# The scan's state decay on VectorE, and ln(dt) in the bias of the mask's exponential

## The chip, the cores and the metric

The kernel runs on one core of a Trainium2 chip. The metric is the device time of one execution in microseconds (us), lower is better; a kernel's time here is the median of its runs.

## The reference, cut to what matters

One step of a one-layer hybrid encoder on 1024 prompt tokens and 64 sample tokens: a large input projection, differential attention, a state-space scan (SSD), two branch projections, an output projection, and a convolutional feed-forward part. The change lies in the scan. Per chunk of tokens it computes:

```python
acum = jnp.cumsum(dtc * a_neg, axis=1)
seg = acum[:, :, None] - acum[:, None, :]
decay = jnp.exp(jnp.where(causal[None, :, :, None, None], seg, -jnp.inf))
xdt = xc * dtc[..., None]
cb = jnp.einsum('blgn,bsgn->blsg', cc, bc)
y = jnp.einsum('blsg,blsge,bsgep->blgep', cb, decay, xdt)
y = y + jnp.einsum('blgn,bgepn->blgep', cc, state) * jnp.exp(acum)[..., None]
to_end = jnp.exp(acum[:, -1:] - acum)
state = state * jnp.exp(acum[:, -1])[..., None, None] + jnp.einsum('blgn,blge,blgep->bgepn', bc, to_end, xdt)
```

There are 32 heads in 4 groups of 8. The time step `dt` multiplies `xc` along the summed token `s`, so it may stand as a factor exp(ln dt) in `decay` just as well.

## The kernel before, in words

The layer is one program. Nearly every large product is split into high and low parts and runs as three TensorE matmuls (lines 170, 171 and 172 of `product`). After the attention comes the scan: `scan()` walks 4 groups, each of three spans (384, 384 and 320 tokens), each span in chunks of 128 tokens (the last chunk of a group is the 64 sample tokens, with a state of its own, `start`). That makes 36 chunks; a chunk's first half (`front`) runs one chunk ahead of its second half (`back`).

`front` transposes the chunk's x on TensorE into a PSUM tile `tr`, has VectorE multiply it by `dt` and by `dtw` in one instruction (L1306, out `xx` = `xdt` and `xw`), lets GpSimd write -1e30 above the diagonal of the decay's exponents `bc` (`affine_select`, L1307), takes eight exponentials on ScalarE with `nacum` as bias (L1309), and multiplies them by C·B on VectorE (L1310). `back` runs the products yi (L1318, from `xdt` and `bc`), ye (L1324, from the state) and the state's update `up` (L1330, from `xw`). VectorE multiplies ye by the outer decay (L1325) and adds yi (L1326). A group's first chunk has no state yet: ScalarE copies yi to y (L1328) and `up` to the new state (L1333). In the other 32 chunks GpSimd multiplies the old state by its decay (L1335), and VectorE adds `up` (L1337). `gated`, `normed` and `scaled` finish a span and store y to DRAM (`y_sc`, L1374 for the first two groups, L1365 for the others). The tile y has two buffers, so the first write to a span's y waits until the store of the span two before it has landed.

TensorE is kept busy between the scan's small products: after each half step `fill(SCAN_STEPS)` takes matmuls of other work, here the gate projections and then the attention and SSM branches (`branch`), whose results VectorE (L234) or ScalarE (L232, L970) takes out of PSUM. All engines run their instructions in the order in which the scheduler put them at build time; it orders by a priority and its own estimate of times, so an edit can move instructions far from its own lines. `steps()` runs once, early in the input projections, and makes `dt_tok`, `nacum`, `decs` and `dtw` for all chunks at once.

Of the kernel before, what the change touches and what calls it, by code (L numbers as in the profile page):

```python
# [9 lines left out]
F32 = mybir.dt.float32  # L10
R32 = mybir.dt.float32r
AF = mybir.ActivationFunctionType
ALU = mybir.AluOpType
# [4 lines left out]
P = 128  # L18
# [71 lines left out]
def hybrid_layer(ctx: ExitStack, tc: tile.TileContext, xT, xt, prm, cst, rope, wvd, win, wbs, wba, wout, wup, wdn,  # L90
                 ckT, cv, st0, yT, kT, v, ssm, conv, ffn):
    nc = tc.nc
    V, S, G, PE = nc.vector, nc.scalar, nc.gpsimd, nc.tensor
    act = S.activation
# [166 lines left out]
    nacum, decs = (dq.tile([P, 9, 32], F32, name=n) for n in ("nacum", "decs"))  # L261
    dtt = dq.tile([P, 2, 9, 32], F32, name="dtt")
    dt_tok, dtw = dtt[:, 0], dtt[:, 1]
# [12 lines left out]
    def stat(w):  # L276
        t = ps1.tile([P, 512], F32, name="st", tag="st")
        return t[:, :w]
# [197 lines left out]
    def row(tag, name, dt=F32):  # L476
        if tag in ("fa", "fs", "fu"):
            w = {"fa": KT * P, "fs": 4 * P, "fu": HT}[tag]
            return rows_l.tile([P, w], dt, name=name, tag=tag, bufs=IN_ROWS[tag])
        w = {"ss": T}.get(tag, HT)  # L480
        return rows_r.tile([P, w], dt, name=name, tag=tag, bufs=IN_ROWS[tag])
# [223 lines left out]
    def steps():  # L705
        flat = [four[:, 288 * i : 288 * (i + 1)] for i in range(3)] + [row("fx", "dt2")[:, :288]]
        da, e, t, t2 = (x.rearrange("p (a b) -> p a b", b=32) for x in flat)
        u = dtw
        act(e, u, AF.Abs)
        act(e, e, AF.Exp, scale=-1.0)  # L710
        V.tensor_scalar_add(t, e, 2.0)
        V.reciprocal(t, t)
        V.tensor_tensor(out=t, in0=t, in1=e, op=ALU.mult)
        V.tensor_tensor(out=t2, in0=t, in1=t, op=ALU.mult)
        yield
        V.tensor_scalar(e, t2, 1.0 / 17, None, ALU.mult)
        for n in (15, 13, 11, 9, 7, 5, 3):
            V.scalar_tensor_tensor(e, e, 1.0 / n, t2, ALU.add, ALU.mult)
        yield
        V.scalar_tensor_tensor(e, e, 1.0, t, ALU.add, ALU.mult)  # L720
        V.tensor_scalar_max(u, u, 0.0)
        V.scalar_tensor_tensor(dt_tok, e, 2.0, u, ALU.mult, ALU.add)
        an = four[:, 864:896]
        act(an, par[:, O_AL : O_AL + 32], AF.Exp)
        V.scalar_tensor_tensor(da, dt_tok, -1.0, an.unsqueeze(1).to_broadcast([P, 9, 32]), ALU.mult, ALU.mult)
        V.memset(da[TS:, 8, :], 0.0)
        yield
        flat = lambda x: x.rearrange("p a b -> p (a b)")
        pa = stat(288)
        with tc.issue_after(seen["mm"].ins):  # L730
            PE.matmul(pa, tri, flat(da), start=True, stop=True)
        V.tensor_scalar(flat(nacum), pa, -1.0, None, ALU.mult)
        yield
        pl = stat(288)
        with tc.issue_after(seen["mm"].ins):
            PE.matmul(pl, ones, flat(da), start=True, stop=True)
        act(flat(decs), pl, AF.Exp)
        V.tensor_tensor(out=flat(dtw), in0=pl, in1=flat(nacum), op=ALU.add)
        act(dtw, dtw, AF.Exp)
        V.tensor_tensor(out=dtw, in0=dtw, in1=dt_tok, op=ALU.mult)  # L740
        yield
        for c, w in WIDE:
            af = row("fc", "af")[:32, :w]
            pf = stat(512)
            with tc.issue_after(seen["mm"].ins):
                for i in range(c // P, -(-(c + w) // P)):
                    n = min(P, T - i * P)
                    PE.matmul(pf[:32, i * P - c : i * P - c + n], da[:n, i], tri[:n, :n], start=True, stop=True)
            V.tensor_copy(af, pf[:32, :w])
            m = (min(c + w, TP) - c) // P  # L750
            load(out=a_sc[c // P : c // P + m].rearrange("c h t -> h c t"), in_=af[:, : P * m].rearrange("h (c t) -> h c t", t=P))
            if c + w > TP:
                load(out=a_sc[8, :, :TS], in_=af[:, P * m : P * m + TS])
            yield
# [510 lines left out]
    with (tc.tile_pool(name="sin", bufs=1) as sin, tc.tile_pool(name="sp", bufs=1) as sp,  # L1265
# [21 lines left out]
        def front(g, ch, o, bx, xs, bc):  # L1287
            L = P if ch < 8 else TS
            cs = slice(o, o + L)
            h8 = slice(8 * g, 8 * g + 8)  # L1290
            e2 = sp.tile([P, 4, P], F32, name="e2", tag="e2", bufs=3)
            for u in range(2):
                half = slice(64 * u, 64 * u + 64)
                act(e2[half, :, :L], bc.rearrange("p (j u) t -> p u j t", u=2)[half, u, :, :L], AF.Exp)
            tr = psi.tile([P, 512], F32, name="tr", tag="tr")
            for j in range(4):
                PE.transpose(tr[:L, P * j : P * (j + 1)], xs[:, j, cs], ident)
            cb = psi.tile([P, 512], F32, name="cb", tag="cb")
            PE.transpose(cb[:L, 0:P], bx[:, 0, cs], ident)
            PE.matmul(cb[:L, P : P + L], bx[:, 0, cs], bx[:, 1, cs], start=True, stop=True)  # L1300
            b_cb = sp.tile([P, 2 * P], F32, name="b_cb", tag="b_cb", bufs=3)
            S.copy(b_cb[:L, : P + L], cb[:L, : P + L])
            xx = sp.tile([P, 2, 8, 64], F32, name="xx", tag="xx", bufs=2)
            xdt, xw = xx[:, 0], xx[:, 1]
            tr3 = tr[:L].rearrange("p (e q) -> p e q", e=8).unsqueeze(1).to_broadcast([L, 2, 8, 64])
            V.tensor_tensor(out=xx[:L], in0=tr3, in1=dtt[:L, :, ch, h8].unsqueeze(3).to_broadcast([L, 2, 8, 64]), op=ALU.mult)  # L1306
            G.affine_select(bc[:L, :, :L], bc[:L, :, :L], [[0, 8], [1, L]], ALU.is_ge, -1e30, base=0, channel_multiplier=-1)  # L1307
            for e in range(8):
                act(bc[:L, e, :L], bc[:L, e, :L], AF.Exp, bias=nacum[:L, ch, 8 * g + e : 8 * g + e + 1])  # L1309
            V.tensor_tensor(out=bc[:L, :, :L], in0=bc[:L, :, :L], in1=b_cb[:L, P : P + L].unsqueeze(1).to_broadcast([L, 8, L]), op=ALU.mult)  # L1310
            return L, cs, bc, e2, b_cb, xdt, xw

        def back(g, ch, bx, y, state, start, L, cs, bc, e2, b_cb, xdt, xw):
            h8 = slice(8 * g, 8 * g + 8)
            yi = psi.tile([P, 4, P], F32, name="yi", tag="yi")
            for e in range(8):
                u = 64 * (e % 2)
                PE.matmul(yi[u : u + 64, e // 2, :L], xdt[:L, e], bc[:L, e, :L], start=True, stop=True)  # L1318
            if ch == 8:
                state = start  # L1320
            if state is not None:
                ye = pss.tile([P, 4, P], F32, name="ye", tag="ye")
                for j in range(4):
                    PE.matmul(ye[:, j, :L], state[:, P * j : P * (j + 1)], bx[:, 1, cs], start=True, stop=True)  # L1324
                V.tensor_tensor(out=y[:, :, cs], in0=ye[:, :, :L], in1=e2[:, :, :L], op=ALU.mult)  # L1325
                V.tensor_tensor(out=y[:, :, cs], in0=y[:, :, cs], in1=yi[:, :, :L], op=ALU.add)  # L1326
            else:
                S.copy(y[:, :, cs], yi[:, :, :L])  # L1328
            up = pss.tile([P, 512], F32, name="stp", tag="stp")
            PE.matmul(up, b_cb[:L, :P], xw[:L].rearrange("p e q -> p (e q)"), start=True, stop=True)  # L1330
            new = sp.tile([P, 512], F32, name="state", tag="state", bufs=2)
            if state is None:
                S.copy(new, up)  # L1333
            else:
                G.tensor_tensor(out=new.rearrange("p (e q) -> p e q", e=8), in0=state.rearrange("p (e q) -> p e q", e=8),  # L1335
                                in1=decs[:, ch, h8].unsqueeze(2).to_broadcast([P, 8, 64]), op=ALU.mult)
                V.tensor_tensor(out=new, in0=new, in1=up, op=ALU.add)  # L1337
            if ch >= 7:
                ends.append((ssm[ch - 7, :, 512 * g : 512 * (g + 1)], new))
            return new  # L1340
# [37 lines left out]
        def scan():  # L1378
# [9 lines left out]
            def begin(n):  # L1388
                if n == len(steps):
                    return None  # L1390
                if n and n + 2 < len(steps):
                    asked.append(ask(*steps[n + 2]))
                i, g, c, w, o = steps[n]
                return front(g, (c + o) // P, o, *got[i], asked[n])
# [592 lines left out]
```

## Time and profile before

| | |
|---|---|
| median of 3 runs | 2413.97 us (2413.55 to 2416.66) |
| the profiled execution | 2411.51 us, of which the span of its instructions is 2409.7 us |
| TensorE busy, share of the span | 98% |
| VectorE, ScalarE, GpSimd busy | 72%, 50%, 26% |
| the scan | from about 1130 to 1475 us of the span |
| TensorE clock granted | 0.999 of full speed |

In rows of the profile PE is TensorE's matmul, PEld its weight load, DVE is VectorE, ACT is ScalarE, POOL is GpSimd and SP the engine that issues DMAs. A row of waits reads: engine, the waiting tile and line, `<-` what released it, then microseconds in total, number of waits, longest wait. A row on a tile reads: line, engine, operation, `x` count, then shortest, median and longest time in ns.

### The profile page before, as it was taken

What the parts mean: (1) busy time and instruction counts of PE and PEld (TensorE: products, weight loads), DVE (VectorE), ACT (ScalarE), POOL (GpSimd) and SP (SyncE); (2) the same over time, 40 slices, a digit from 0 to 9 for tenths busy, and PEclk for the clock granted to TensorE, in tenths of its full rate; (3) what the DMA queues carried; (4) which work ended last, traced back from release to release, by engine and by line L of the source; (5) the groups of instructions that cost most, each with busy time, mean ns of one, the idle gap of its engine ahead of it and who ended that gap; (6) DMA issues with size and microseconds to landing.
All of it is one profiled execution on the core that took longest, in us unless ns stands there. A gap on an engine that the chain in (4) does not pass through costs nothing. (4 is left out here: it accounts for less than half of the span.)

```text
span 2409.7 us, 48636 instructions
## 1 busy us (share of the span) xinstructions
PE 2373.4 (98%) x18649; PEld 2302.2 (96%) x18649; DVE 1729.4 (72%) x2938; ACT 1201.2 (50%) x2600; POOL 634.4 (26%) x689
## 2 busy tenths in 40 slices
PE   8999999999999999999999999999999999999998
PEld 8999999999999999999898889999899999999998
DVE  4678887646858768884898886647866667677765
ACT  6444454335656656665566664334443343353442
POOL 0032443320100000001223220012254455443444
PEclk9999999999999999999999999999999999999999
DMA  7873768526554444435978956663124324357876
GB/s 246 273 245 129 266 221 303 170 102 208 160 156 161 151 144 137 148 110 188 353 266 280 331 192 205 203 215 130 65 82 164 138 98 162 127 191 211 246 184 106
DMA packets 288170, 449.74 MB, mean 187 GB/s; under 512 B 35833, under 2 KB 178306, under 8 KB 287938
## 3 DMA queue, kind: packets, MB, share of 16 engines
q1 hardware_dynamic: 258594, 387.00, 48.6%
q0 software_dynamic: 11040, 26.34, 5.4%
q10 hardware_dynamic: 18304, 33.30, 3.7%
q8 instruction: 147, 2.41, 0.4%
q14 instruction: 85, 0.70, 0.1%
HBM read 294.03 MB, written 152.50 MB: 185 GB/s over the span
## 5 line engine op out<-in xcount | busy, mean ns | idle before, releaser
L170 PE MATMUL mm<-b,w_hi 128*128 128x272 f32 x1376 | 407.7, 296 | 0.0
L171 PE MATMUL mm<-b,w_hi 128*128 128x272 f32 x1376 | 405.8, 295 | 0.0
L172 PE MATMUL mm<-b,w_lo 128*128 128x272 f32 x1376 | 403.8, 294 | 0.0
L171 PEld LDWEIGHTS mm<-b,w_hi 128*128 128x128 f32 x1376 | 259.5, 189 | 5.9 <-issue 4.1
L170 PEld LDWEIGHTS mm<-b,w_hi 128*128 128x128 f32 x1376 | 259.3, 188 | 5.3 <-issue 2.7
L172 PEld LDWEIGHTS mm<-b,w_lo 128*128 128x128 f32 x1376 | 259.0, 188 | 5.2 <-issue 4.2
L1629 PE MATMUL mx<-m,w_hi 128*128 128x272 f32 x792 | 152.3, 289 | 2.5 <-DVE hb L1667 1.3
L420 DVE TENSOR_TENSOR wh<-w_f,wh 128x512 fp32r<-128x512 f32 (+1 forms) x156 | 149.7, 960 | 0.7 <-ACT wh L419 0.7
L1629 PE MATMUL mx<-n,wh 128*128 128x272 f32 x1056 | 141.7, 288 | 1.3 <-DVE u L1656 0.9
L1629 PEld LDWEIGHTS mx<-n,wh 128*128 128x128 f32 x1056 | 135.7, 188 | 1.7 <-DVE u L1656 1.2
L1132 ACT ACTIVATE p_t<-sc,mx 128x512 f32<-128x512 f32 (+6 forms) x144 | 106.0, 739 | 59.0 <-DVE mx L1123 33.0
L1629 PEld LDWEIGHTS mx<-m,w_hi 128*128 128x128 f32 x792 | 124.4, 188 | 2.9 <-DVE hb L1667 1.5
L170 PE MATMUL mx<-b,w_hi 128*128 128x272 f32 x416 | 123.4, 297 | 1.1 <-ACT w_hi L155 0.8
L172 PE MATMUL mx<-b,w_lo 128*128 128x272 f32 x416 | 121.6, 294 | 0.0
L563 POOL TENSOR_TENSOR ws<-w_f 128x512 f32<-128x512 f32 (+1 forms) x51 | 69.0, 1354 | 195.4 <-DMA w_f<-in_wdn_dram 84.2
L171 PE MATMUL mx<-b,w_hi 128*128 128x272 f32 x416 | 120.4, 290 | 0.0
L1009 DVE SCALAR_TENSOR_TENSOR cc<-pre,par,cc 128x544 f32<-128x544 f32 (+1 forms) x144 | 111.2, 772 | 8.2 <-ACT cc L1007 6.9
L156 DVE TENSOR_TENSOR w_lo<-w_f,w_hi 128x1024 fp32r<-128x1024 f32 (+1 forms) x74 | 92.5, 1251 | 33.9 <-ACT w_hi L155 33.7
L1629 PE MATMUL mx<-m,w_lo 128*128 128x272 f32 x396 | 114.2, 289 | 0.0
L1638 ACT ACTIVATE cc<-pre,par 128x544 f32<-128x544 f32 (+1 forms) x44 | 37.2, 846 | 150.0 <-DVE pre L1673 149.1
L419 ACT CAST wh<-w_f 128x512 fp32r<-128x512 f32 (+1 forms) x156 | 95.3, 613 | 26.1 <-POOL w_f L569 6.8
L155 ACT CAST w_hi<-w_f 128x1024 fp32r<-128x1024 f32 (+1 forms) x74 | 77.6, 1049 | 56.1 <-PE mm L171 30.3
(466 smaller groups left out, 7124.8 us busy)
## 6 DMA issues: line engine op xcount, KB each, us to landing
w_f<-in_win_dram SPq DMA_DIRECT2D x40, 512.0 KB, 3.9
w_f<-in_wup_dram SPq DMA_DIRECT2D x80, 256.0 KB, 2.6
w_f<-in_win_dram SPq DMA_DIRECT2D x76, 256.0 KB, 3.2
bc<-a_sc SPq DMA_DIRECT2D x32, 512.0 KB, 7.0
b<-y_sc SPq DMA_DIRECT2D x24, 544.0 KB, 8.2
h_sc<-hb SPq DMA_DIRECT2D x44, 272.0 KB, 2.1
ht<-h_sc SPq DMA_DIRECT2D x22, 544.0 KB, 4.6
t_sc<-ht SPq DMA_DIRECT2D x22, 544.0 KB, 3.0
```

Of the source, the lines that this page charges most:

```text
L155: S.copy(hi, w)
L156: V.tensor_tensor(out=lo, in0=w, in1=hi, op=ALU.subtract)
L170: PE.matmul(ps, a_hi, b_hi, start=i == 0, stop=False)
L171: PE.matmul(ps, a_hi, b_lo, start=False, stop=False)
L172: PE.matmul(ps, a_lo, b_hi, start=False, stop=i == n - 1)
L419: S.copy(hi, src)
L420: V.tensor_tensor(out=lo, in0=src, in1=hi, op=ALU.subtract)
L563: G.tensor_tensor(out=s1, in0=q21, in1=q22, op=ALU.add)
L1009: V.scalar_tensor_tensor(cc[:, :m], pre[:, i : i + m], cw(i), cc[:, :m], ALU.mult, ALU.add)
L1132: act(p_t[:n, :nk], sc[c][:n, :nk], AF.Exp, bias=mx[:n, c : c + 1], accum_out=dst)
L1629: PE.matmul(ps, w[x][:, c], b[y][:, k], start=start and k == i == 0, stop=k == 3 and i == 2, skip_group_check=not start)
L1638: act(cc[:, :n], pre[h][:, :n], AF.Identity, bias=col(O_FB + f), scale=cw(0))
```

## The change: what it does

```diff
--- before.py
+++ after.py
@@ -738,6 +738,9 @@
         V.tensor_tensor(out=flat(dtw), in0=pl, in1=flat(nacum), op=ALU.add)
         act(dtw, dtw, AF.Exp)
         V.tensor_tensor(out=dtw, in0=dtw, in1=dt_tok, op=ALU.mult)
+        V.tensor_scalar_max(dt_tok, dt_tok, 1e-37)
+        act(dt_tok, dt_tok, AF.Ln)
+        V.tensor_tensor(out=nacum, in0=nacum, in1=dt_tok, op=ALU.add)
         yield
         for c, w in WIDE:
             af = row("fc", "af")[:32, :w]
@@ -1302,8 +1305,9 @@
             S.copy(b_cb[:L, : P + L], cb[:L, : P + L])
             xx = sp.tile([P, 2, 8, 64], F32, name="xx", tag="xx", bufs=2)
             xdt, xw = xx[:, 0], xx[:, 1]
-            tr3 = tr[:L].rearrange("p (e q) -> p e q", e=8).unsqueeze(1).to_broadcast([L, 2, 8, 64])
-            V.tensor_tensor(out=xx[:L], in0=tr3, in1=dtt[:L, :, ch, h8].unsqueeze(3).to_broadcast([L, 2, 8, 64]), op=ALU.mult)
+            tr3 = tr[:L].rearrange("p (e q) -> p e q", e=8)
+            S.copy(xdt[:L], tr3)
+            V.tensor_tensor(out=xw[:L], in0=tr3, in1=dtw[:L, ch, h8].unsqueeze(2).to_broadcast([L, 8, 64]), op=ALU.mult)
             G.affine_select(bc[:L, :, :L], bc[:L, :, :L], [[0, 8], [1, L]], ALU.is_ge, -1e30, base=0, channel_multiplier=-1)
             for e in range(8):
                 act(bc[:L, e, :L], bc[:L, e, :L], AF.Exp, bias=nacum[:L, ch, 8 * g + e : 8 * g + e + 1])
@@ -1318,7 +1322,10 @@
                 PE.matmul(yi[u : u + 64, e // 2, :L], xdt[:L, e], bc[:L, e, :L], start=True, stop=True)
             if ch == 8:
                 state = start
+            new = sp.tile([P, 512], F32, name="state", tag="state", bufs=2)
             if state is not None:
+                V.tensor_tensor(out=new.rearrange("p (e q) -> p e q", e=8), in0=state.rearrange("p (e q) -> p e q", e=8),
+                                in1=decs[:, ch, h8].unsqueeze(2).to_broadcast([P, 8, 64]), op=ALU.mult)
                 ye = pss.tile([P, 4, P], F32, name="ye", tag="ye")
                 for j in range(4):
                     PE.matmul(ye[:, j, :L], state[:, P * j : P * (j + 1)], bx[:, 1, cs], start=True, stop=True)
@@ -1328,12 +1335,9 @@
                 S.copy(y[:, :, cs], yi[:, :, :L])
             up = pss.tile([P, 512], F32, name="stp", tag="stp")
             PE.matmul(up, b_cb[:L, :P], xw[:L].rearrange("p e q -> p (e q)"), start=True, stop=True)
-            new = sp.tile([P, 512], F32, name="state", tag="state", bufs=2)
             if state is None:
                 S.copy(new, up)
             else:
-                G.tensor_tensor(out=new.rearrange("p (e q) -> p e q", e=8), in0=state.rearrange("p (e q) -> p e q", e=8),
-                                in1=decs[:, ch, h8].unsqueeze(2).to_broadcast([P, 8, 64]), op=ALU.mult)
                 V.tensor_tensor(out=new, in0=new, in1=up, op=ALU.add)
             if ch >= 7:
                 ends.append((ssm[ch - 7, :, 512 * g : 512 * (g + 1)], new))
```

Three edits. In `steps()`, `dt_tok` is raised to at least 1e-37, replaced by its logarithm, and added to `nacum`; so the exponentials of the mask carry the factor dt. In `front`, `xdt` is then the plain transposed x, copied out of PSUM by ScalarE, and VectorE makes `xw` alone, in half the elements. In `back`, the multiplication of the old state by its decay moves from GpSimd to VectorE and in front of the sums of y. GpSimd keeps the `affine_select`. The tile `new` is now taken ahead of the products of the state, in every chunk.

The scheduler gives new orders to all engines within the scan; TensorE's instructions are the same in number, and their order outside the scan is unchanged. In rows of the order, what stands in brackets is whose progress the instruction waits for (Activation is ScalarE, Pool GpSimd, DMAHW a DMA queue). VectorE at the second and third chunk of the first group, before:

```order
L1325 TENSOR_TENSOR y<-ye,e_14151 128x4x128 [waits PE_49]
L1310 TENSOR_TENSOR bc<-bc,b_cb 128x1024 [waits Activation_49,Pool_49]
L1337 TENSOR_TENSOR state<-state,stp 128x512 [waits PE_49,Pool_49]
L1326 TENSOR_TENSOR y<-y,yi 128x4x128 [waits DVE_49,PE_49]
L1306 TENSOR_TENSOR xx<-tr,dtt 128x1024
L1325 TENSOR_TENSOR y<-ye,e_14260 128x4x128 [waits PE_49]
L1310 TENSOR_TENSOR bc<-bc,b_cb 128x1024 [waits Activation_49,Pool_49]
L1337 TENSOR_TENSOR state<-state,stp 128x512 [waits PE_49,Pool_49]
L1326 TENSOR_TENSOR y<-y,yi 128x4x128 [waits DVE_49,PE_49]
L1306 TENSOR_TENSOR xx<-tr,dtt 128x1024 [waits PE_49]
```

One row on `xx` per chunk makes `xdt` and `xw` together and waits for TensorE at most or, behind others, for nothing; the state's sum waits for GpSimd. The same place now, where L1310 is the new product for `xw`, L1314 the product with the mask, L1327 the state's decay, L1332 and L1333 the sums of y, and L1341 the state's sum:

```order
L1332 TENSOR_TENSOR y<-ye,e_14155 128x4x128 [waits PE_49]
L1314 TENSOR_TENSOR bc<-bc,b_cb 128x1024 [waits Activation_49,Pool_49]
L1341 TENSOR_TENSOR state<-state,stp 128x512 [waits DVE_49,PE_49]
L1310 TENSOR_TENSOR xx<-tr,dtt 128x512 [waits Activation_49]
L1327 TENSOR_TENSOR state<-state,decs 128x512 [waits DVE_49]
L1333 TENSOR_TENSOR y<-y,yi 128x4x128 [waits PE_49]
L1314 TENSOR_TENSOR bc<-bc,b_cb 128x1024 [waits Activation_49,Pool_49]
L1332 TENSOR_TENSOR y<-ye,e_14265 128x4x128 [waits PE_49]
L1310 TENSOR_TENSOR xx<-tr,dtt 128x512 [waits Activation_49]
L1341 TENSOR_TENSOR state<-state,stp 128x512 [waits DVE_49,PE_49]
L1327 TENSOR_TENSOR state<-state,decs 128x512 [waits DVE_49]
L1333 TENSOR_TENSOR y<-y,yi 128x4x128 [waits PE_49]
```

Each row on `xx` has half the elements and now waits for ScalarE, whose copy reads the same PSUM tile; the state's decay is a row more; the state's sum no longer waits for GpSimd.

ScalarE where the third group begins, around the copy of its first chunk's y (L1328 before, L1335 now; `b_cb` is a copy from PSUM, `bc` the exponentials, `e_...` the outer decay, `zin` a cast or a square for the finished span), before:

```order
L256 ACTIVATE gn_16618<-gn_16619 128x320 [waits Activation_49]
L1302 COPY b_cb<-cb 128x256 [waits PE_49]
L1370 CAST zin<-y 128x2x320 [waits DVE_49] x2
L1302 COPY b_cb<-cb 128x256 [waits PE_49]
L1328 COPY y<-yi 128x4x128 [waits DMAHW3_49]
L1294 ACTIVATE e_16788<-bc 64x512 [waits DMAHW6_49,DVE_49]
L1294 ACTIVATE e_16788<-bc 64x512
L1302 COPY b_cb<-cb 128x256 [waits PE_49]
```

The y copy (L1328) stands behind a `b_cb` copy and a cast and waits for one DMA queue. Now, where L1309 is the new copy of `xdt` and L1339 the state's copy:

```order
L1297 ACTIVATE e_16519<-bc 64x512 [waits DMAHW5_49,DVE_49]
L1297 ACTIVATE e_16519<-bc 64x512
L1305 COPY b_cb<-cb 128x256 [waits PE_49]
L1313 ACTIVATE bc<-bc,nacum 128x128 [waits Pool_49]
L1313 ACTIVATE bc<-bc,nacum 128x128 [waits Activation_49]
L1309 COPY xx<-tr 128x512 [waits PE_49]
L1313 ACTIVATE bc<-bc,nacum 128x128 x6
L1339 COPY state<-stp 128x512 [waits DMAHW7_49,DMAHW6_49,PE_49]
L1335 COPY y<-yi 128x4x128 [waits DMAHW3_49,DVE_49,PE_49]
L1350 ACTIVATE zin<-y 128x4x320 [waits DMAHW4_49,DVE_49]
L1309 COPY xx<-tr 128x512 [waits PE_49]
```

The y copy waits for a DMA in both, and behind it there now stands a copy of `xdt` for which VectorE waits. In TensorE's order, 87 gate and branch matmuls stood between the yi products of this group's first two chunks, and now 15 do.

## The prediction

> **What bounds the kernel now.** I read the page's head first, then the busy time by stretch, then who waited for whom in the scan.
>
> ```profile
> span 2409.7 us, 48636 instructions
> PE 2373.4 (98%) x18649; PEld 2302.2 (96%) x18649; DVE 1729.4 (72%) x2938; ACT 1201.2 (50%) x2600; POOL 634.4 (26%) x689
> ```
>
> TensorE is busy for 98% of the span. The change works in the scan alone, so the question is what TensorE waits for there. The stretches (length, then busy time of PE, PEld, DVE, ACT and POOL):
>
> ```profile
> 1130.00:1475.00 345.00, 341.76 (x2781) 306.35 (x2780) 287.51 (x377) 215.65 (x521) 90.78 (x68) 1.00 0.82 276
> 1200.00:1320.00 120.00, 120.00 (x981) 108.40 (x980) 111.16 (x155) 79.93 (x185) 37.65 (x24) 1.00 0.80 266
> 1320.00:1440.00 120.00, 116.76 (x961) 104.24 (x961) 94.94 (x119) 76.65 (x189) 29.78 (x24) 1.00 0.81 280
> ```
>
> In the scan's 345 us TensorE lacks 345.00 - 341.76 = 3.2 us. VectorE has 345.00 - 287.51 = 57.5 us of idle time there, ScalarE 129.4, GpSimd 254.2. VectorE is nearest to a bound between 1200 and 1320 us, where it has only 120.00 - 111.16 = 8.8 us left. The waits of the scan name the 3.2 us:
>
> ```profile
> PE yi L1318 <- ACT y L1328: 1.9, 1, 1.9
> PE tr L1297 <- DMA in<-x_sc: 0.7, 1, 0.7
> PE yi L1318 <- DVE y L1326: 0.6, 1, 0.6
> ```
>
> Three waits in 36 chunks, 1.9 + 0.7 + 0.6 = 3.2 us. GpSimd's share in the old chain looks large, but nothing of it arrives at TensorE:
>
> ```profile
> POOL bc L1307 <- ACT e L1294: 146.4, 28, 28.9
> POOL state L1335 <- DVE state L1337: 77.4, 15, 12.6
> ACT bc L1309 <- POOL bc L1307: 16.0, 16, 3.3
> DVE state L1337 <- PE stp L1330: 1.3, 2, 1.1
> ```
>
> GpSimd waits for the others (146.4 and 77.4 us), and the VectorE sum behind its state decay (L1337) never waits for GpSimd in these rows, only 1.3 us for TensorE. So the decay that is moved was hidden, and **no gain can be larger than about 3.2 us (0.13%)**, as long as the order of TensorE's own work costs the same. It should: in the scan's order the gate and branch matmuls are interrupted by scan products 105 times before and 104 times after.
>
> **The change part by part.** In `steps()`, three more operations on 128x288, once. Their nearest rows are:
>
> ```profile
> L738 DVE TENSOR_TENSOR dtt<-st,nacum x1: 452/452/452, 215.4 to 215.4; 128x288 f32<-128x288 f32 x1
> L739 ACT ACTIVATE dtt<-dtt x1: 447/447/447, 216.3 to 216.3; 128x288 f32<-128x288 f32 x1
> 180.00:240.00 60.00, 59.37 (x454) 57.11 (x453) 48.45 (x84) 29.82 (x59) 14.09 (x11) 1.00 0.38 131
> ```
>
> Two on VectorE and one on ScalarE, 3 x 0.45 = 1.4 us in a row. TensorE's next products of `steps()` read `da` and not their results, VectorE has 11.5 of 60 us free there: 0 on the path, 1.4 us if that cover is gone. The order has no more table loads on ScalarE than before, so the logarithm adds none.
>
> In the scan, the rows that price the rest (shortest, median, longest ns):
>
> ```profile
> L1306 DVE TENSOR_TENSOR xx<-tr,dtt x36: 1206/1216/1226, 1128.8 to 1454.1; 128x1024 f32<-128x1024 f32 x32, 64x1024 f32<-64x1024 f32 x4
> L1337 DVE TENSOR_TENSOR state<-state,stp x32: 669/676/689, 1145.2 to 1469.4; 128x512 f32<-128x512 f32 x32
> L1310 DVE TENSOR_TENSOR bc<-bc,b_cb x36: 672/1214/1920, 1136.3 to 1456.7; 128x1024 f32<-128x1024 f32 x32, 64x512 f32<-64x512 f32 x4
> L1333 ACT COPY state<-stp x4: 561/567/589, 1140.0 to 1392.0; 128x512 f32<-128x512 f32 x4
> L1335 POOL TENSOR_TENSOR state<-state,decs x28: 1037/1047/3618, 1140.7 to 1454.3; 128x512 f32<-128x512 f32 x28
> ```
>
> VectorE's `xw`: 512 elements with one operand in PSUM, as L1337: 36 x (0.676 - 1.216) = -19.4 us. Its new state decay: 32 times 512 elements. The lower price is again L1337's 0.676; the upper one comes from L1310, whose operands both lie in SBUF as the decay's do and whose longest time is 1920/1214 = 1.58 times its median: 1.07 us. So 32 x 0.676 = +21.6 us, at most 32 x 1.07 = +34.2 us. I take the lower, since L1310's median is the undisturbed 1214. VectorE's sum: **+2.2 us** in 345, at most +14.8. By chunks (36 in 345 us) a third of it falls between 1200 and 1320 us: 0.8 us, at most 5.1, of the 8.8 free. It does not fill VectorE up.
>
> [...]
>
> ScalarE's copy of `xdt`: 36 x 0.567 = **+20.4 us** out of 129.4 idle. It takes a place in front of the exponentials, so it can delay them by 0.57 us a chunk; between yi and its chunk's transposes stand tens of matmuls at the usual spacing. GpSimd: some 32 x 1.05 us less at the median, worth nothing on the path.
>
> **The new wait.** `xw` now waits for ScalarE's copy, since both read the tile `tr`. Behind it on VectorE stand the state's decay, the sums of y and the branch results that free TensorE's PSUM banks. Rows of VectorE waiting for ScalarE today:
>
> ```profile
> DVE w_lo L156 <- ACT w_hi L155: 10.4, 5, 3.6
> DVE bc L1310 <- ACT bc L1309: 5.9, 5, 2.7
> ```
>
> From these, a wait costs 5.9/36 = 0.16 us per chunk, and if L156's mean wait of 2.1 us met every chunk, 36 x 2.1 = 75 us, more than VectorE's 57.5 idle. I take the nearer row, L1310, which also waits once per chunk on a ScalarE result made shortly before: 6 us in all, inside the 57.5.
>
> [...]
>
> [...]
>
> **The sum.** On the path: steps 0, decay 0, copy 0, new wait 0 so far as VectorE's idle time covers it; existing waits 3.2 us, of which the order may remove or move any. I add +0.5 us, a judgement between -3.2 and the first rival's price, since ScalarE and VectorE now wait for each other once more per chunk. The profiled execution took 2411.51 us with 1.8 us outside its span; with +0.5 it would take 2412.0. The median of the runs, 2413.97, lies 2.5 us above it, so I forecast **2414.5 us**.
>
> **The rivals.** *Slower: the y store.* The longest wait of TensorE has this origin:
>
> ```profile
> 1301.12 0.29 PE L170 MATMUL mm<-b,w_hi 128*128 128x272 f32 x1
> 1302.26 0.29 PE L170 MATMUL mm<-b,w_hi 128*128 128x272 f32 x1
> 1310.76 0.94 DVE L1371 TENSOR_TENSOR y<-y,zin 128x768 fp32r<-128x768 f32 x1
> 1324.23 0.59 ACT L1328 COPY y<-yi 128x512 f32<-128x512 f32 x1 [4.97 <-DMA y_sc<-y]
> 1324.87 1.09 PE L1318 MATMUL yi<-bc,xx 128*64 128x128 f32 x16 [1.89 <-ACT y L1328]
> DVE y L1325 <- DMA y_sc<-y: 5.2, 2, 2.9
> ```
>
> ScalarE's y copy at the third group's start waited 4.97 us for the store of y, whose last part VectorE finished at 1311.70; that is 12.5 us. TensorE had 87 matmuls (9 take 1302.26 - 1301.12 = 1.14 us, so 0.127 each, 11 us) between that chunk's yi and the next and still waited 1.89 us. Now 15 stand there, 1.9 us, and behind the y copy waits ScalarE's `xdt` copy, behind that VectorE's `xw`. If the store lands as late as before relative to its products, TensorE loses up to 11 - 1.9 = 9 us: 2423. It decides from the point where the store lands more than some 2 us behind the yi product of that group's first chunk. Against it: the scheduler also puts that span's last products earlier, before the yi product of the group before's last chunk, and 5.2 us in 2 waits on VectorE cost TensorE only 0.6 us. The same pattern on VectorE could return at other span ends.
>
> *Faster: the waits go.* If ScalarE's exponentials no longer wait the 16.0 us for GpSimd's mask, and the y sums come early enough, all 3.2 us vanish: 2413.97 - 3.2 = 2410.8. That is still within 0.2%. For a larger gain nothing in these rows has room.
>
> *VectorE full.* With the upper decay price and a wait of 1 us a chunk, the stretch from 1200 to 1320 us gets 5.1 + 12.5 = 17.6 us for 8.8 free, so some 9 us would stay on the path: 2423. The row of L1337 and the mean of L1310's waits speak against it.
>
> **How the numbers follow.** About 0.2%, 4.8 us, is what a measurement of this kernel can tell from no change. Hidden as forecast, with 0 to 4 us of new small waits or some of the 3.2 us gone: 0.76, split 0.56 for the forecast and 0.20 for the waits going. The y store: 0.13, VectorE full: 0.07; both lie above 2418.8. Faster by over 0.2% would need something these rows do not show: 0.04. The low end is the forecast of all waits gone, 2410.8; the high end takes in most of both slower cases at 2422.0.
>
> **What would show it.** Right: TensorE still within 3 to 5 us of full in the scan; `xw` near 680 ns, 36 `xdt` copies near 570 ns, decays near 680 to 700; VectorE's waits for ScalarE before `xw` below 10 us. Wrong: a TensorE wait of several us on yi at the third group's start with ScalarE's y copy named (the y store), or TensorE waits on VectorE's branch results between 1200 and 1320 us (VectorE full), or a change of time outside the scan.

## The result and the profile after

The changed kernel takes 2421.28 us (median of 10 runs, 2412.33 to 2423.28) against 2413.15 us for the kernel before (10 runs): ratio 1.0024, 95% interval 1.0012 to 1.0035. A second measurement on another occasion gave 2418.78 against 2412.74, ratio 1.0025 (1.0015 to 1.0035). So the change costs 8.1 and 6.0 us by the medians, about 0.25% by both ratios. The forecast was 2414.5 us with a range from 2410.8 to 2422.0; the time lies in the range, but on the slower side, to which the prediction gave a chance of 0.20.

The head of the page of the changed kernel:

```profile
span 2420.8 us, 48654 instructions
PE 2381.3 (98%) x18649; PEld 2308.9 (95%) x18649; DVE 1730.1 (71%) x2972; ACT 1217.8 (50%) x2637; POOL 586.8 (24%) x657
```

VectorE's busy time is what it was (1729.4 before), ScalarE has 16.6 us more, GpSimd 47.6 us less. None of the three explains a longer span. Where the time went is read from two rows on tiles: the scan's first transposition (tile `tr`) and the last product of the last span's sums of squares (tile `gst`). Behind the three durations stand the first and the last start, in us. Before, then after:

```profile
L1297 PE MATMUL tr<-con,in x144: 270/273/332, 1121.7 to 1452.9; 128*128 128x128 f32 x128, 128*64 128x128 f32 x16
L1352 PE MATMUL gst<-zin,con x24: 431/484/590, 1168.8 to 1481.3; 128*128 128x384 f32 x16, 128*128 128x320 f32 x8
```

```profile
L1300 PE MATMUL tr<-con,in x144: 269/273/331, 1122.9 to 1463.2; 128*128 128x128 f32 x128, 128*64 128x128 f32 x16
L1356 PE MATMUL gst<-zin,con x24: 430/486/591, 1169.3 to 1491.6; 128*128 128x384 f32 x16, 128*128 128x320 f32 x8
```

From the first of the one to the last of the other the scan takes 1481.3 - 1121.7 = 359.6 us before and 1491.6 - 1122.9 = 368.7 us after: 9.1 of the 11.1 us by which the two spans differ; 1.2 us of the rest stand ahead of the scan and 0.8 behind it. TensorE's waits in the changed kernel's scan, all that the view lists from 1122.8 to 1491.7 us:

```profile
PE mm L170 <- ACT w_hi L155: 1.7, 1, 1.7
PE cb L1302 <- ACT b_cb L1305: 1.7, 2, 1.0
PE yi L1322 <- ACT y L1335: 1.0, 1, 1.0
PE mm L172 <- DVE w_lo L156: 0.6, 1, 0.6
PE yi L1322 <- DVE bc L1314: 0.6, 1, 0.6
PE mx L170 <- ACT w_hi L155: 0.4, 1, 0.4
PE tr L1300 <- DVE xx L1310: 0.4, 1, 0.4
PE tr L1300 <- DMA in<-x_sc: 0.3, 1, 0.3
PE mx L172 <- DVE w_lo L156: 0.2, 1, 0.2
```

They sum to 6.9 us, where 3.2 us stood before. No single wait is large; eight of the nine rows name ScalarE or VectorE. The longest comes near 1345 us: TensorE wants the weights of a branch, and ScalarE's casts of them (`w_hi`, L155) stand behind a chunk's exponentials (L1313), which themselves waited for GpSimd's mask (2.30 us long there, where its median is 1.09). VectorE made the `xw` of that stretch at 1341.55 without any wait. ScalarE's timeline there, then TensorE's (start, length, engine, line, and in brackets the idle time ahead and what ended it):

```profile
1339.89 0.37 ACT L1305 COPY b_cb<-cb 128x256 f32<-128x256 f32 x1
1342.26 2.45 ACT L1313 ACTIVATE bc<-bc,nacum 128x128 f32<-128x128 f32 x8 [2.00 <-POOL bc L1311]
1344.62 1.98 ACT L155 CAST w_hi<-w_f 128x1024 fp32r<-128x1024 f32 x2
1345.70 0.39 PE L170 MATMUL mm<-b,w_hi 128*128 128x272 f32 x1 [1.68 <-ACT w_hi L155]
1346.65 0.39 PE L170 MATMUL mx<-b,w_hi 128*128 128x272 f32 x1 [0.43 <-ACT w_hi L155]
1348.05 0.60 PE L172 MATMUL mm<-b,w_lo 128*128 128x272 f32 x1 [0.62 <-DVE w_lo L156]
```

From 1347.3 us on, behind the first two of these waits and during the third, TensorE's granted clock is at half. The stretches of the changed kernel (length, busy time of PE, PEld, DVE, ACT and POOL, granted clock, DMA share, GB/s):

```profile
1200.00:1320.00 120.00, 119.61 (x966) 107.09 (x964) 102.69 (x152) 78.15 (x179) 14.61 (x12) 1.00 0.77 258
1320.00:1440.00 120.00, 116.34 (x924) 104.48 (x926) 93.70 (x135) 83.04 (x200) 17.44 (x13) 0.97 0.86 290
```

```profile
1348.00:1354.00 6.00, 5.95 (x26) 5.96 (x27) 5.55 (x8) 0.85 (x2) 0.00 (x0) 0.50 1.08 384
```

TensorE is "busy" for 5.95 of those 6.00 us but gets through 26 matmuls, 0.229 us each, where 0.127 is usual. A mean clock of 0.97 over 120 us is about 0.03 x 120 = 3.6 us. So of the 9.1 us, 6.9 - 3.2 = 3.7 are waits and some 3.6 the clock behind them; the other 2 are neither, and what they are stays open.

The clock episode isn't needed for the verdict. In the profiled execution of the second measurement no half clock shows there (the stretch from 1320 to 1440 us has 1.00), and these rows give 1488.4 - 1123.6 = 364.8 us, still 5.2 more than before:

```profile
L1300 PE MATMUL tr<-con,in x144: 270/272/330, 1123.6 to 1460.1; 128*128 128x128 f32 x128, 128*64 128x128 f32 x16
L1356 PE MATMUL gst<-zin,con x24: 430/486/590, 1168.8 to 1488.4; 128*128 128x384 f32 x16, 128*128 128x320 f32 x8
```

Last, the new instructions of the changed kernel, from the views of their tiles:

```profile
L1309 ACT COPY xx<-tr x36: 557/578/605, 1132.4 to 1463.8; 128x512 f32<-128x512 f32 x32, 64x512 f32<-64x512 f32 x4
L1310 DVE TENSOR_TENSOR xx<-tr,dtt x36: 672/680/692, 1133.0 to 1465.8; 128x512 f32<-128x512 f32 x32, 64x512 f32<-64x512 f32 x4
L1327 DVE TENSOR_TENSOR state<-state,decs x28: 672/683/1492, 1144.5 to 1464.3; 128x512 f32<-128x512 f32 x28
```

And the wait that the change adds, from the waits of all engines in the scan:

```profile
DVE xx L1310 <- ACT xx L1309: 12.7, 7, 3.9
```

The durations came out as forecast, and the two readers of `tr` run one behind the other: the first copy starts at 1132.4, the first `xw` at 1133.0. VectorE waits 12.7 us for ScalarE's copy, in 7 of 36 chunks, where 6 us was forecast (9.4 us in the second profiled execution); and that is now the suspect. ScalarE itself is held in front of its copy, too, until TensorE has made `tr` or a yi product:

```profile
ACT xx L1309 <- PE tr L1300: 12.3, 5, 5.4
ACT xx L1309 <- PE yi L1322: 4.8, 1, 4.8
```

### The profile page after: what moved, and what is told of

Same layout as the page of the kernel before. It is cut to its first block, busy times and chain, and to the rows that moved or that the text cites. A ratio compares the mean times of both kernels' runs of the same rounds, so it can differ in the third digit from the quotient of the medians.

```text
span 2420.8 us, 48654 instructions
## 1 busy us (share of the span) xinstructions
PE 2381.3 (98%) x18649; PEld 2308.9 (95%) x18649; DVE 1730.1 (71%) x2972; ACT 1217.8 (50%) x2637; POOL 586.8 (24%) x657
## 4 chain that ended last, share of the span: by engine, by line
PE 50%; DVE 4%; DMA 4%; issue 2%; ACT 1%; SPq 0%; POOL 0%; POOLq 0%; DVEq 0%; ACTq 0%
PE mx L1633 13%; PE mx L1807 6%; PE mm L1633 5%; PE mm L172 3%; PE mm L170 3%; PE mm L171 3%; PE mx L170 2%; PE mx L172 2%; PE mx L171 2%; PE mm L1807 2%; PE po L1170 1%; PE yi L1322 1%; PE stp L1337 1%; PE ye L1331 1%; DMA y_sc<-y 1%
## 5 line engine op out<-in xcount | busy, mean ns | idle before, releaser
L1311 POOL TENSOR_SCALAR_AFFINE_SELECT bc<-bc 128x1024 f32<-128x1024 f32 (+1 forms) x36 | 44.0, 1223 | 306.0 <-ACT e L1297 232.9
```

## The experiments

The theories were: (A) ScalarE's new copy of `xdt`, for which VectorE waits, is what makes other results late for TensorE; (B) the decay crowds VectorE; (C) it is the clock, by chance. The first runs measured the changed kernel again, each half alone, and the copy on the other engine.

**The changed kernel again.** No edit.

> The changed kernel once more, for the granted clock of every run beside that of the kernel before. Theory A (ScalarE's new copy of xdt, on which VectorE now waits, makes casts and exponentials late for TensorE): +5 to +9 us against the kernel before, with the mean granted clock below that of before in most runs. Theory B (the state's decay crowds VectorE): the same +5 to +9. Theory C (the difference is in the granted clock alone and comes by chance): both kernels show the same spread of clocks, and at equal clock the times agree within 2 us.

2418.78 us against 2412.74 (35 runs of before), ratio 1.0025 (1.0015 to 1.0035). The loss repeats. Theory C alone is out: among the executions with a mean granted clock of 0.998, four of this kernel took 2418.2 us on average and fourteen of the kernel before 2411.8. The clock is a part of it at most: over all executions its mean is 0.9969 here and 0.9978 before, and 0.0009 x 2413 = 2 us.

**The logarithm and the copy alone.** The decay stays on GpSimd, in its old place:

```diff
-            new = sp.tile([P, 512], F32, name="state", tag="state", bufs=2)
             if state is not None:
-                V.tensor_tensor(out=new..., in0=state..., in1=decs[...], op=ALU.mult)
...
+            new = sp.tile([P, 512], F32, name="state", tag="state", bufs=2)
...
+                G.tensor_tensor(out=new..., in0=state..., in1=decs[...], op=ALU.mult)
                 V.tensor_tensor(out=new, in0=new, in1=up, op=ALU.add)
```

> The edits in steps() and in front alone: ln(dt) in the bias, xdt copied by ScalarE, xw alone on VectorE; the state's decay stays on GpSimd in its old place. Theory A: most of the loss is here, +5 to +9 us. Theory B: no loss, VectorE gets 19 us lighter, -2 to +2 us. Theory C: any value from -2 to +8, going with the clock.

2417.30 us, ratio 1.0023 (1.0010 to 1.0035), +4.6 us.

**The decay on VectorE alone.** The other half: `steps()` and `front` as before, `back` as after.

```diff
-        V.tensor_scalar_max(dt_tok, dt_tok, 1e-37)
-        act(dt_tok, dt_tok, AF.Ln)
-        V.tensor_tensor(out=nacum, in0=nacum, in1=dt_tok, op=ALU.add)
...
-            S.copy(xdt[:L], tr3)
-            V.tensor_tensor(out=xw[:L], in0=tr3, in1=dtw[...], op=ALU.mult)
+            V.tensor_tensor(out=xx[:L], in0=tr3, in1=dtt[...], op=ALU.mult)
```

> The edit in back alone: the state's decay on VectorE in front of the sums of y; front and steps() as before. VectorE gets 32 x 0.68 = 22 us more work. Theory A: little, -2 to +2 us. Theory B: the loss is here, +5 to +9 us, with TensorE waits on VectorE between 1200 and 1320 us. Theory C: any value from -2 to +8, going with the clock.

2414.96 us, ratio 1.0009 (0.9997 to 1.0022), +2.2 us with an interval that holds no change, and in its trace TensorE waits for VectorE nowhere between 1200 and 1320 us, as B would have it. Most of the loss comes with the other half.

**The copy on VectorE.** The changed kernel with one word of `front` changed:

```diff
-            S.copy(xdt[:L], tr3)
+            V.tensor_copy(xdt[:L], tr3)
```

> The changed kernel with the copy of xdt on VectorE instead of ScalarE: no wait of VectorE on ScalarE for it, ScalarE's load as before, VectorE some 0.4 to 0.7 us a chunk (14 to 24 us in all) heavier. Theory A: the loss goes, -2 to +3 us. Theory B: the loss grows, +8 to +15 us. Theory C: any value from -2 to +8, going with the clock.

2415.90 us, ratio 1.0015 (1.0001 to 1.0028), +3.2 us. By this measurement about half of the loss goes, although VectorE now has a copy more (0.680 us per chunk at the median); that speaks against B, but not all went. The next runs asked for the rest, and whether the copy alone costs in the kernel before.

**The logarithm just ahead of the scan.** The changed kernel; its three operations on `dt_tok` leave `steps()`:

```diff
-        V.tensor_scalar_max(dt_tok, dt_tok, 1e-37)
-        act(dt_tok, dt_tok, AF.Ln)
-        V.tensor_tensor(out=nacum, in0=nacum, in1=dt_tok, op=ALU.add)
... (ahead of the scan)
+        V.tensor_scalar_max(dt_tok, dt_tok, 1e-37)
+        act(dt_tok, dt_tok, AF.Ln)
+        V.tensor_tensor(out=nacum, in0=nacum, in1=dt_tok, op=ALU.add)
```

> The changed kernel with the three operations of ln(dt) moved from steps(), early in the input projections, to a place just before the scan. If they cost TensorE time where they stood (waits for VectorE and ScalarE at 125, 318 and 419 us that the trace of before has shorter or not at all), 1 to 2 us of the loss go: +4 to +6 us against the kernel before, where the changed kernel stood at +6.0. If the loss is ScalarE's copy and the wait on it alone, nothing goes: +5 to +7 us.

2419.03 us against 2413.17 (27 runs), ratio 1.0021 (1.0012 to 1.0030). But the edit did not move the work: the scheduler left the three operations where they were, some 900 us ahead of the scan (the maximum started at 217.7 us in the changed kernel):

```profile
L1379 DVE TENSOR_SCALAR dtt<-dtt x1: 1277/1277/1277, 218.6 to 218.6; 128x288 f32<-128x288 f32 x1
```

Every compute engine's instructions stand in the changed kernel's order in this trace. So the run says nothing of the place of the logarithm; it is a third measurement of the changed kernel, and the loss is there again, +5.9 us.

**Both.** The edit above and the copy on VectorE together. Here too the three operations ran at 218.6 us, and every compute engine has the order of the run with the copy on VectorE alone.

> Both mends: the copy of xdt on VectorE, and the three operations of ln(dt) just before the scan. copy_dve stood at +3.2 us with a scan 1.7 us shorter than before's in its profiled run. If both terms add up: -1 to +2 us against the kernel before. If the loss is in the scheduler's new order whatever it is made of: +2 to +5 us.

2412.10 us, ratio 0.9999 (0.9989 to 1.0009): the kernel before's time, with the decay still on VectorE in its new place. That fells B. It is a second measurement of one and the same order: +3.2 us and -1.1 us, 4.2 us apart, though the intervals, 1.0001 to 1.0028 and 0.9989 to 1.0009, barely overlap. So two measurements can differ by that much, and a single difference of 2 to 4 us here can't be told from none.

**The new place, on GpSimd.** The kernel before, with its decay on GpSimd moved in front of the sums of y:

```diff
+            new = sp.tile([P, 512], F32, name="state", tag="state", bufs=2)
             if state is not None:
+                G.tensor_tensor(out=new..., in0=state..., in1=decs[...], op=ALU.mult)
...
-            new = sp.tile([P, 512], F32, name="state", tag="state", bufs=2)
...
-                G.tensor_tensor(out=new..., in0=state..., in1=decs[...], op=ALU.mult)
```

> The kernel before with the state's decay written in front of the sums of y, still on GpSimd: no engine gets other work, only the place in the program and with it the scheduler's order changes. If the loss needs work on another engine (theory A or B): -1 to +1 us. If any new order of the scan costs some us because the old one happened to be a good one: +2 to +6 us.

2410.72 us, ratio 0.9989 (0.9980 to 0.9998), 2.5 us below before: not every new order of the scan costs several us.

**The copy alone, in the kernel before.** Per chunk a ScalarE copy of the transposed tile into `xw`, which VectorE's product then writes over:

```diff
+            S.copy(xw[:L], tr[:L].rearrange("p (e q) -> p e q", e=8))
             tr3 = ...
             V.tensor_tensor(out=xx[:L], in0=tr3, in1=dtt[...], op=ALU.mult)
```

> The kernel before with one more copy of tr by ScalarE in every chunk, into the place that VectorE then overwrites with xw; so VectorE's product waits for ScalarE as in the changed kernel, VectorE and GpSimd keep their work, and steps() is as before. Theory A: +3 to +7 us, most of the loss. If ScalarE's copy and the wait are hidden: -1 to +1 us.

2422.08 us, ratio 1.0038 (1.0023 to 1.0052), +8.9 us, above the range of theory A, with neither the logarithm nor the decay on VectorE. Its mean granted clock is 0.9948 against 0.9979, which by 0.0031 x 2413 would be 7.5 us of it; around the ends of its two longest new waits of TensorE, 5.3 us on `gst` to 1487.7 us and, behind the scan, 4.4 us on `w_hi` to 1529.0, the granted clock is 0.78 (1487 to 1500 us) and 0.76 (1528 to 1540). A copy on ScalarE brings two things, though: half a microsecond of work in front of ScalarE's other work, and a wait of VectorE. The last runs were to take them apart.

**The two readers of `tr` in the other order.** The changed kernel, two lines exchanged:

```diff
-            S.copy(xdt[:L], tr3)
             V.tensor_tensor(out=xw[:L], in0=tr3, in1=dtw[...], op=ALU.mult)
+            S.copy(xdt[:L], tr3)
```

> The changed kernel with its two readers of the transposed tile in the other order: VectorE makes xw first, ScalarE copies xdt behind it. VectorE no longer waits for ScalarE there; ScalarE waits for VectorE instead, and has the same 36 copies. If VectorE's wait for ScalarE is what costs, the time falls back to within 2.5 us of before. If ScalarE's work or its coupling to VectorE in either direction costs, it stays 4 to 9 us above before. If the clock by chance is the cause, it stays near the changed kernel, +6.

2411.93 us against 2412.21 (29 runs), ratio 0.9998 (0.9990 to 1.0007). The whole loss is gone. ScalarE's copies are as many and as long as in the changed kernel; what is turned round is who waits, and with it the scheduler's order, TensorE's too. Rows of this kernel on tiles: the copy, and the scan's first and last products:

```profile
L1310 ACT COPY xx<-tr x36: 561/581/593, 1132.2 to 1456.8; 128x512 f32<-128x512 f32 x32, 64x512 f32<-64x512 f32 x4
L1300 PE MATMUL tr<-con,in x144: 270/273/332, 1123.8 to 1455.0; 128*128 128x128 f32 x128, 128*64 128x128 f32 x16
L1356 PE MATMUL gst<-zin,con x24: 432/486/561, 1170.3 to 1481.9; 128*128 128x384 f32 x16, 128*128 128x320 f32 x8
```

Its new wait, from the waits of all engines in the scan:

```profile
ACT xx L1310 <- DVE xx L1309: 15.9, 9, 4.0
```

ScalarE waits 15.9 us for VectorE, more than the 12.7 us that VectorE had waited for ScalarE and about as long as ScalarE had been held by TensorE in the changed kernel (12.3 + 4.8 = 17.1 us); so it does not cost by itself that ScalarE is held so long. The scan takes 1481.9 - 1123.8 = 358.1 us. TensorE's waits in it:

```profile
PE tr L1300 <- ACT xx L1310: 1.2, 1, 1.2
PE gst L1356 <- DVE zin L1352: 0.8, 1, 0.8
PE tr L1300 <- DMA in<-x_sc: 0.6, 1, 0.6
```

2.6 us in all, less than the 3.2 of before; the late weights and late `b_cb` are gone.

**The wait without the work.** The kernel before, with a ScalarE copy of one column:

```diff
+            S.copy(xw[:L, 0, 0:1], tr[:L, 0:1])
             tr3 = ...
             V.tensor_tensor(out=xx[:L], in0=tr3, in1=dtt[...], op=ALU.mult)
```

> The kernel before, and per chunk a ScalarE copy of one column of the transposed tile into xw, which VectorE overwrites: the wait of VectorE on ScalarE without the half microsecond of ScalarE's work. If the wait is what costs, +5 to +9 us on before, like the full copy (+8.9). If ScalarE's work in front of its casts and exponentials costs, within 3 us of before.

2426.07 us, ratio 1.0061 (1.0046 to 1.0075), +13.9 us: above the range expected, and dearer than the full copy. The copy's row:

```profile
L1305 ACT COPY xx<-tr x36: 133/153/166, 1130.3 to 1467.7; 128x1 f32<-128x1 f32 x32, 64x1 f32<-64x1 f32 x4
```

VectorE's wait for it and TensorE's longest waits in the scan:

```profile
DVE xx L1307 <- ACT xx L1305: 12.9, 7, 3.5
PE mx L172 <- DVE w_lo L156: 3.5, 1, 3.5
PE cb L1299 <- ACT xx L1305: 2.8, 1, 2.8
```

36 copies of 0.153 us are 5.5 us of work on ScalarE, and again VectorE waits some 13 us in 7 chunks. TensorE's waits again name a weight's low part from VectorE and a PSUM tile that ScalarE hadn't yet taken out. Neither stands next to a wait of VectorE for the copy. The 3.5 us end at 1187.3 us, and VectorE's last such wait had ended at 1140.5; from 1176 to that point VectorE had no idle time at all, and `w_lo` was behind other work. The 2.8 us end at 1305.7, behind a wait of ScalarE for the DMA that loads a chunk's exponents:

```profile
1303.57 1.27 ACT L1294 ACTIVATE e<-bc 64x512 f32<-64x512 f32 x2 [3.42 <-DMA bc<-a_sc]
```

The edit is also not the wait of VectorE alone: the copy holds ScalarE until TensorE has made `tr`.

```profile
ACT xx L1305 <- PE tr L1297: 14.8, 7, 5.3
```

**The work without the wait.** The kernel before, with a ScalarE copy that nobody reads:

```diff
+            spare = sp.tile([P, 4, 112], F32, name="spare", tag="spare", bufs=1)
+            S.copy(spare[:, :, : min(L, 112)], xs[:, :, cs.start : cs.start + min(L, 112)])
             tr3 = ...
```

> The kernel before, and per chunk a ScalarE copy of 448 columns of x into a spare tile that nobody reads, at the place of the copy of xdt: ScalarE's work without anyone waiting for it. If ScalarE's work in front of its casts and exponentials costs, +4 to +9 us on before. If VectorE's wait costs, within 3 us of before.

2415.22 us, ratio 1.0012 (1.0003 to 1.0020), +3.0 us, at the bound set for the other theory. Its 36 copies have a median of 0.566 us, near the 0.578 of the changed kernel's. They read x and not `tr`, so they wait for no product of TensorE, but for the load of x they do, 12.2 us in all. A difference of 3 us is within what two measurements of one order differ by; whether the work costs anything by itself is open (in the kernel above, with the readers exchanged, it cost nothing), but it is not the 6 to 14 us of the kernels in which VectorE waits.

**The new place on GpSimd, once more.**

> The kernel before with the state's decay still on GpSimd but in front of the sums of y, once more. If the small gain of its first measurement (-2.5 us) is real, it is again 1 to 4 us below before; if it was scatter, within 1 us of it.

2413.32 us, ratio 1.0001 (0.9993 to 1.0010), +1.1 us. The small gain did not repeat; the two measurements, 3.6 us apart, show neither a cost nor a gain of this place. No kernel here beats the kernel before.

## Why the prediction was right or wrong

**In the range by luck.** The forecast for the most likely case was +0.5 us, and +8.1 and +6.0 were measured. The time lies below the high end of 2422.0 only because that end was set for two rivals, the y store and a full VectorE, and neither came. VectorE's wait in front of `xw` was to stay below 10 us; it was 12.7 us in one profiled execution and 9.4 in the other.

**Right: no gain is to be had.** TensorE was bound, its waits in the scan were 3.2 us, and no variant came more than 2.5 us below before, nor that one twice.

**Right: the durations and VectorE's sum.** `xw` took 0.680 us (0.676 forecast), the decay 0.683 (0.676), so 36 x (0.680 - 1.216) + 32 x 0.683 = +2.6 us against +2.2. The upper price of 1.07 us, an estimate from L1310's longest time, did not come: the median is 0.683 with single ones up to 1.49. ScalarE's copies took 0.578 (0.567). VectorE had 102.69 of 120 us busy between 1200 and 1320 us, so it did not fill up, and that rival is out.

**Right in the sum, wrong in a row: `steps()`.** The three operations were to take 1.4 us; in the changed kernel the maximum alone took 1.28:

```profile
L741 DVE TENSOR_SCALAR dtt<-dtt x1: 1278/1278/1278, 217.7 to 217.7; 128x288 f32<-128x288 f32 x1
L742 ACT ACTIVATE dtt<-dtt x1: 440/440/440, 220.6 to 220.6; 128x288 f32<-128x288 f32 x1
L743 DVE TENSOR_TENSOR nacum<-nacum,dtt x1: 448/448/448, 221.7 to 221.7; 128x288 f32<-128x288 f32 x1
```

2.17 us in all, and hidden, as said: the kernel with the readers exchanged, which has these three operations in `steps()`, is as fast as before.

**Wrong: the step "I add +0.5 us, a judgement".** The mechanism was named, ScalarE and VectorE wait for each other once more per chunk, and the new wait of VectorE stood where it was expected, in front of `xw`. The price of the new dependence was what failed. The wait was put at 6 us and held to be hidden by VectorE's 57.5 us of idle time, with below 10 us as the mark of being right; it measured 12.7. But the size isn't the error that counts: 15.9 us of the opposite wait cost nothing, and 9.4 us went with a loss of 6.0. The error was to take the cost of the new dependence from VectorE's idle time alone, and to leave out what the whole order becomes when ScalarE's read of `tr` stands in front of VectorE's: TensorE's waits in the scan grew from 3.2 to 6.9 us, with some 3.6 us of clock behind them. With the two reads exchanged they are 2.6 us. Whether VectorE's idle time covered the wait itself is not shown either way. The term measured +6.0 to +8.1 us at the medians, not +0.5, about what the prediction gave its rivals.

**Wrong: "existing waits 3.2 us, of which the order may remove or move any".** The order of TensorE's own work was weighed by its count of switches, 105 against 104, and that count did not show whether weights and PSUM tiles come in time. The old waits did go or shrink (1.9 to 1.0 on yi behind the y copy), and 1.7 + 1.7 + 0.6 + 0.6 + 0.4 + 0.4 + 0.2 = 5.6 us of others came, of kinds that were not in the scan before: the `w_hi` and `w_lo` of a branch, `b_cb`, the product with the mask, `tr`.

**Wrong: the clock taken as steady.** The waits were priced at their own length. In the profiled execution waits of 1.68, 0.43 and 0.62 us within some 4 us went with 6.8 us at half clock, about 3.6 us by the mean of 0.97, more than their own 2.73 us again.

**The slower rival was another one.** The y store was to cost up to 9 us at the third group's start. ScalarE's y copies waited for the store of y for 2.7 us in all, where one waited 4.97 before:

```profile
ACT y L1335 <- DMA y_sc<-y: 2.7, 1, 2.7
```

TensorE lost 1.0 us to such a copy in the whole scan. That is the wait at the third group's start, at 1320.9 us; with 15 matmuls left between the products, no more than this 1.0 us was lost to the store as it now landed.

**What is shown, and what is not.** Shown, by programs that differ in a line or two: it costs to have ScalarE read `tr` in front of VectorE. The changed kernel lost 8.1, 6.0 and 5.9 us in three measurements, and 4.6 us with the decay left on GpSimd; such a read put into the kernel before cost 8.9 us, and 13.9 even where ScalarE's work is 0.153 us. With the two reads exchanged and the work kept the loss is gone, and with both reads on VectorE it is +3.2 and -1.1 us.

Not shown: the way from VectorE's wait to TensorE's late weights. The longest waits of TensorE looked at do not stand behind a wait of VectorE for the copy: in the changed kernel ScalarE's casts stood behind GpSimd's mask, in the kernel with one column `w_lo` stood behind other work of VectorE and `b_cb` behind a late load, and in the kernel with the full copy added the longest in the scan is 5.3 us on `gst`, at its very end. The rival that stands untested is the order itself: the scheduler writes all orders anew for every edit, TensorE's in the scan too, and a program with this dependence may simply get a worse one. How much is time lost while the chip runs, and how much is the order, wasn't separated; it would need kernels with their order held fixed.

## What to carry to other kernels

When a result with one reader gets two readers on two engines, and they run one behind the other, measure both orders: the same work with two lines exchanged was worth 6 to 8 us here. Do not price the new wait by the waiting engine's idle time: 12.7 us of waits went with a loss, 15.9 us of the opposite ones with none. Where a scheduler makes the order anew, look in the trace whether the lines that an edit moves have moved at all; here the logarithm had not. Measure one order twice before reading a difference of 2 to 4 us out of 2413. Removing work from an engine whose waits do not reach TensorE, as GpSimd's 47.6 us here, brought nothing.

## What the runs showed of the hardware

Short waits of TensorE can be followed by a stretch at half clock: granted clock 0.50 from 1347.3 to 1354.1 us of the changed kernel's profiled execution, behind waits of 1.68 and 0.43 us and during one of 0.62, and 0.229 us per matmul in place of 0.127. None of TensorE's waits in that scan was longer than 1.7 us. Such waits also came without it: in the profiled execution of the second measurement, of the same kernel, the same three rows of waits are 1.3, 0.4 and 0.6 us, and the granted clock is 1.00 from 1320 to 1440 us. So what such waits bring with them in clock varies between executions.

A maximum with a constant on 128x288 took 1.28 us on VectorE, where a sum of two tensors of that size took 0.448. GpSimd was at work during the first (a product of 1.38 us from 217.45 us, another of 1.36 from 218.79) and not during the second, at 221.7 us. The two operations differ as well, and no run here shows what makes the difference; nothing depended on it.
